# A hybrid decoder block on one core: latents loaded tile by tile over 13 slots, query evacuations in a row, other banks for the last unit's transposes

## The chip, the cores and the metric

The kernel runs on one core of a Trainium2 chip. The metric is the device time of one execution in microseconds (us); lower is better. Before the change the median of three runs is 906.58 us, between 903.97 and 908.92.

The engines are TensorE (PE, with its weight loads as PEld), VectorE (DVE), ScalarE (ACT), GpSimd (POOL) and SyncE (SP), whose queue issues nearly all transfers (DMAs). Each runs its own instructions in a fixed order; a wait of one instruction holds all behind it.

## The reference, cut to what matters

One layer on a sequence of 1024 tokens, width 1024, in float32. A normalised and modulated input is projected once; the parts of the projection feed two groups of heads.

```python
h = rms_norm(x, norm_g) * (1 + scale) + shift
proj = h @ w_in                                        # (1024, 3360)
y_rwkv = rwkv7_time_mix(proj[..., :1664], ...)         # 8 heads of 64: a recurrence over the tokens
q  = (rms_norm(c_q,  q_norm_g)  @ w_uq).reshape(..., 8, 96)   # c_q: 384 columns of proj
kv = (rms_norm(c_kv, kv_norm_g) @ w_ukv).reshape(..., 8, 128) # c_kv: 256 columns of proj
y_mla = causal softmax attention of 8 heads (64 + 32 rotary)
y = concat(y_rwkv * silu(gate_r), y_mla * silu(gate_m))
out = rms_norm(x + gate * (y @ w_out), final_g)
```

`c_q` and `c_kv` are the latents: low-rank tensors from which all queries, keys and values are made. The change is about how they are brought back from DRAM and used.

## The kernel before, in words

Large matrix products take three matmuls: each float32 operand is split into a rounded part (`h`, hi) and a rest (`l`, lo), and hi*hi, lo*hi and hi*lo are added in PSUM. A split is a cast on ACT (`split_to`, L787) and a subtraction on DVE (L790).

The work up to the attention is one loop over step groups `n` = 0 to 10 with `STEPS[n]` steps `j` each (L1019 to L1035). Each step issues pieces of the recurrence and then, by a rate per group (`RATE`), pieces of a filler that keeps PE busy:

- The recurrence is cut into 8 units, each two head pairs on 256 tokens. A unit is prepared (`prep`, `products`, `invert`), fetched and turned (`fetch`, `turn_kb`, `turn_v`, `tmat`), run through `chain` in four sequential steps of small matmuls (L690, L697, L709, L712) with evacuations on ACT, and finished in `post`: the group norm, transposes into the PSUM tile `ytps` (L761), and the affine map on ACT (L764). `invert` is a serial row of 62 small DVE instructions on a PSUM tile `W` (L609, L611), with its input `N` and output `d_w` moved through DRAM.
- The filler (`filler`) projects 24 tiles of 128 columns (`proj`, 2 halves of 24 matmuls, L165 to L167) into two PSUM banks, tag `mm`. The last ones are the latents (`latent`, evacuated into `craw` and stored to `d_c`) and four gate tiles (`evac_gate`: `tg` on ACT, L234, and DVE, L235). Then `values` makes the rotary queries (`qrope`, tiles `qrps`), the values (tiles `vps`) and the first head pair's keys and queries (`heads_qk`, tiles `qkps`).

Staging tiles of 128x512 come from one pool and tag, `e2`, with three buffers (`etile`): the evacuations of the projections, the latents read back (`cr`) and raw weights (`wqr`) all share them. Tiles of one tag are handed out in turn. A second tag of that pool, `p2`, has two buffers (`ys`, `y2`, `bv`, `gr` of `post`, and `dg` of the latents).

`latents` is a generator called twice. At (n, j) = (7, 20) it closes the left pools, loads and splits all of `cq` (three tiles of two halves, `load_c`) and loads `wqr`, the raw rotary query weights. At (8, 6) it loads and splits `ckv` (two tiles of two halves); its halves are first scaled by the row norms, which four small matmuls spread over the partitions (`dg`, `rps`, L802 to L805). It then sets `turned`, for which the filler waits before it starts `values`.

The planner of the framework orders the instructions of each engine: greedily by the order in which the program issued them, as their inputs and tile buffers come free in its model of the machine. `tc.high_priority(offset=...)` moves instructions ahead in that order; `tc.issue_after(ins)` puts the instructions of a block behind `ins` on its engine. Engines that touch one PSUM bank are ordered against each other.

PSUM has eight banks: two of `psM` (tag `mm`) and six of `psA` (`rp` twice, `rc`, `ry`, `rt`, `w`). `ytps` uses `rt`, but in the last unit (n = 7) it uses `mm`. After the loop both pools are closed, and the attention's `psQ` (`op`, `qk`) and `psB` (`s`, `tp`) take the banks.

The attention loops over 64 tiles (head pair, head, block of 128 queries): scores `sp`, a maximum, exponentials, transposes, and the product with the values. During a pair, `heads_qk` makes the next pair's keys and queries through one bank `qk`: an ACT cast of 64 rows (L851) and a DVE subtraction (L852) for each of the two heads.

## Time and profile before

| What | us |
|---|---|
| median of three runs (lowest, highest) | 906.58 (903.97, 908.92) |
| the profiled execution | 912.47 |
| its span, first to last instruction | 910.4 |
| PE busy in it | 825.5 (91%) |
| DVE, ACT, POOL busy | 558.5, 487.7, 306.6 |
| latents read back (`cr`), first and last issue | 493.3, 547.1 |
| first scores of the attention | 634.4 |

Rows of the profile name the engine, the line (L165 is line 165 of the kernel), the operation, the tile written and the tiles read, and the shape. In a timeline the first two numbers are the start and the duration in us, and the bracket gives how long the engine stood idle just before and what released it. In a table of stretches each engine has its busy time and its number of instructions; PEclk is the share of TensorE's full clock that was granted. The projections are over at about 586 us, the filler at 626 us; the attention runs from there to 813 us, and the output projection closes the kernel.

### The profile page before, as it was taken

The page shows a single profiled execution, that of the slowest core. Times are in us where ns is not written, and L with a number is a line of the kernel's source. Part 1 is how long each engine was busy: PE and PEld are TensorE (multiplying, and loading weights), DVE is VectorE, ACT ScalarE, POOL GpSimd, SP SyncE. Part 2 cuts the span into 40 slices and gives each one's busy share as a digit, 9 for nine tenths or more (in the row PEclk, how much of TensorE's full clock was granted, in tenths as well). Part 3 has the DMA queues.
Part 4 walks back from the last instruction along what each step waited for, and adds up shares of the span by engine and source line. Part 5 has one row for each costly group of instructions (what it writes and reads, how often), then busy time and mean ns, then how long its engine had stood idle before and what let it go on. Part 6 is the DMA issues. An engine that isn't in the chain of part 4 may idle for free.

```text
span 910.4 us, 16433 instructions
## 1 busy us (share of the span) xinstructions
PE 825.5 (91%) x5764; PEld 637.2 (70%) x5764; DVE 558.5 (61%) x1450; ACT 487.7 (54%) x1136; POOL 306.6 (34%) x359
## 2 busy tenths in 40 slices
PE   1798999989999999899999889997999998989996
PEld 1586777767767776576667667665777776868785
DVE  5795438367675653866666445266887877764532
ACT  2655223444564746337454563555788887772332
POOL 2311414131414321433332302234445544454440
PEclk9999989999999999999999769998899999999998
DMA  8765434523354333343333423257102121027234
GB/s 265 241 194 157 139 99 130 140 77 116 102 178 121 106 86 105 114 117 107 95 99 116 113 87 105 78 185 167 45 21 65 50 91 47 1 72 241 70 107 148
DMA packets 130562, 104.56 MB, mean 115 GB/s; under 512 B 40488, under 2 KB 108336, under 8 KB 130480
## 3 DMA queue, kind: packets, MB, share of 16 engines
q1 hardware_dynamic: 128368, 98.27, 36.6%
q0 software_dynamic: 960, 3.15, 1.7%
q10 hardware_dynamic: 1152, 2.10, 0.6%
q8 instruction: 46, 0.75, 0.4%
q14 instruction: 36, 0.29, 0.1%
HBM read 75.42 MB, written 28.05 MB: 114 GB/s over the span
## 4 chain that ended last, share of the span: by engine, by line
PE 57%; DVE 11%; ACT 11%; DMA 9%; issue 5%; POOL 4%; SPq 2%; POOLq 0%; DVEq 0%; ACTq 0%
PE mm L165 9%; PE mm L166 8%; PE mm L167 8%; DMA wor<-in_w_out 3%; PE gps L559 2%; ACT pr L1092 2%; PE tp L1103 2%; ACT PTh L1112 2%; PE rc L690 1%; PE rc L697 1%; PE rc L709 1%; DVE PTl L1113 1%; PE po L1166 1%; PE po L1167 1%; PE po L1165 1%
## 5 line engine op out<-in xcount | busy, mean ns | idle before, releaser
L165 PE MATMUL mm<-hTh,whi 128*128 128x512 f32 (+1 forms) x384 | 166.5, 433 | 1.3 <-DVE tg L235 1.3
L166 PE MATMUL mm<-hTl,whi 128*128 128x512 f32 (+1 forms) x384 | 156.2, 407 | 0.0
L167 PE MATMUL mm<-hTh,wlo 128*128 128x512 f32 (+1 forms) x384 | 156.1, 407 | 0.0
L158 POOL TENSOR_TENSOR wlo<-wraw,whi 128x512 fp32r<-128x512 f32 (+1 forms) x54 | 70.6, 1309 | 218.6 <-ACT whi L157 209.7
L165 PEld LDWEIGHTS mm<-hTh,whi 128*128 128x128 f32 (+1 forms) x384 | 72.8, 190 | 21.8 <-DVE tg L235 1.5
L167 PEld LDWEIGHTS mm<-hTh,wlo 128*128 128x128 f32 (+1 forms) x384 | 72.8, 190 | 17.1
L166 PEld LDWEIGHTS mm<-hTl,whi 128*128 128x128 f32 (+1 forms) x384 | 72.9, 190 | 15.5 <-issue 1.9
L1096 POOL TENSOR_SCALAR pr<-pr,sm 128x512 f32<-128x512 f32 (+2 forms) x96 | 55.2, 584 | 78.2 <-DVE sm L1093 49.7
L1092 ACT ACTIVATE pr<-sp,mx,rss 128x128 f32<-128x128 f32 (+3 forms) x64 | 53.4, 834 | 16.0 <-DVE mx L1085 12.9
L1113 DVE TENSOR_TENSOR PTl<-tp,PTh 128x512 fp32r<-128x512 f32 (+2 forms) x96 | 52.3, 554 | 12.8 <-ACT PTh L1112 11.1
L157 ACT CAST whi<-wraw 128x512 fp32r<-128x512 f32 (+1 forms) x54 | 32.7, 607 | 48.8 <-PE mm L166 37.2
L1084 DVE TENSOR_REDUCE mx<-sp 128x1 f32<-128x128 f32 (+3 forms) x64 | 48.1, 751 | 17.2 <-PE sp L1078 17.0
L609 DVE TENSOR_TENSOR wtmp<-W,N 128x60 f32<-128x60 f32 (+24 forms) x248 | 51.2, 206 | 10.2 <-ACT W L604 4.7
L611 DVE TENSOR_TENSOR W<-W,wtmp 128x60 f32<-128x60 f32 (+24 forms) x248 | 53.3, 215 | 5.7
L720 ACT ACTIVATE ST<-rc,eL 64x64 f32<-64x64 f32 x120 | 37.1, 309 | 29.8 <-PE rc L709 28.1
L1112 ACT CAST PTh<-tp 128x512 fp32r<-128x512 f32 (+2 forms) x96 | 44.1, 478 | 15.1 <-PE tp L1103 12.2
L1165 PE MATMUL po<-wo,yh 128*128 128x512 f32 x128 | 50.3, 393 | 0.8 <-ACT od L1139 0.8
L1166 PE MATMUL po<-wo,yh 128*128 128x512 f32 x128 | 50.4, 394 | 0.7 <-DVE wo L790 0.7
L1103 PE MATMUL tp<-cstt,pr 128*128 128x128 f32 x288 | 45.8, 280 | 5.1 <-DVE PTl L1113 2.7
L1167 PE MATMUL po<-wo,yl 128*128 128x512 f32 x128 | 50.3, 393 | 0.0
L1124 PE MATMUL op<-PTh,Vt 128*128 128x256 f32 (+1 forms) x160 | 41.9, 293 | 5.1 <-ACT od L1139 5.1
L1074 PE MATMUL sp<-kt,qt 96*128 96x512 f32 (+2 forms) x96 | 37.2, 388 | 3.0 <-ACT pr L1092 3.0
(282 smaller groups left out, 1973.7 us busy)
## 6 DMA issues: line engine op xcount, KB each, us to landing
wraw<-in_w_in SPq DMA_DIRECT2D x52, 256.0 KB, 3.3
wa<-in_w_ada SPq DMA_DIRECT2D x64, 128.0 KB, 3.4
xt<-in_x SPq DMA_DIRECT2D x8, 512.0 KB
wg<-in_w_ada SPq DMA_DIRECT2D x32, 128.0 KB, 2.7
N<-d_n SPq DMA_DIRECT2D x32, 128.0 KB, 2.7
wor<-in_w_out SPq DMA_DIRECT2D x16, 256.0 KB, 2.9
d_c<-craw SPq DMA_DIRECT2D x10, 256.0 KB, 3.0
cr<-d_c SPq DMA_DIRECT2D x10, 256.0 KB, 3.3
```

The lines of the kernel that those rows point to most:

```text
L158: G.tensor_tensor(lo[:, :, :m], raw[:, :, :m], hi[:, :, :m].bitcast(F32), ALU.subtract)
L165: T.matmul(ps[:m], lhsT=hi[:, k % 4, :m], rhs=a, start=first, stop=False)
L166: T.matmul(ps[:m], lhsT=hi[:, k % 4, :m], rhs=b, start=False, stop=False)
L167: T.matmul(ps[:m], lhsT=lo[:, k % 4, :m], rhs=a, start=False, stop=last)
L1092: A.activation(pr[:, 0:n], sp[:, 0:n], AF.Exp, scale=rss[:, i:i + 1], bias=mx[:], accum_out=sm[:])
L1096: G.tensor_scalar(pr[:, a:e], pr[:, a:e], sm[:], 1.0, ALU.mult, ALU.mult)
L1103: T.transpose(tp[:, j, :], pr[:, (j0 + j) * P:(j0 + j + 1) * P], ident)
L1112: A.copy(th[:, 0:m, bs], tp[:, 0:m])
L1113: V.tensor_tensor(tl[:, 0:m, bs], tp[:, 0:m], th[:, 0:m, bs].bitcast(F32), ALU.subtract)
L1165: T.matmul(ps, lhsT=yh[k][:, ts_], rhs=hi, start=first, stop=False)
L1166: T.matmul(ps, lhsT=yh[k][:, ts_], rhs=lo, start=False, stop=False)
L1167: T.matmul(ps, lhsT=yl[k][:, ts_], rhs=hi, start=False, stop=last)
```

## The change

Three edits.

- **Latents.** `load_c` becomes a generator. It loads one half tile, ends its slot, and splits the half loaded the slot before. For `cq` the raw halves come from a pool of their own, `crp`, with two buffers, which is closed behind them; for `ckv` they stay in `e2`. `latents` then takes 13 calls: six loads and a last split of `cq`, four loads and a last split of `ckv`, and `wqr`. The list `LAT` gives the 13 places, from (7, 20) to (8, 14); `turned` is set at the last. The weights `wqr` are asked for behind `ckv`, no longer ahead of it. Loads, casts and subtractions are the same in number.
- **Evacuations of `heads_qk`.** Both casts are issued ahead of both subtractions, where each cast was followed by its subtraction. This holds for all four head pairs.
- **Transposes of the last unit.** `ytps` of unit 7 uses bank `rt` for the first pair and bank `w` for the second, in place of the two `mm` banks.

```diff
+LAT = ((7, 20), (7, 21), (7, 23), (8, 0), (8, 1), (8, 3), (8, 6), (8, 7), (8, 8), (8, 10), (8, 11), (8, 12), (8, 14))
...
-            ps = (psM if last else psA).tile([64, 4, P], F32, tag="mm" if last else "rt", name="ytps",
-                                            bufs=2 if last else 1)
+            ps = psA.tile([64, 4, P], F32, tag="w" if last and q else "rt", name="ytps", bufs=1)
...
     def load_c(n, base, nm):
         cpool[nm] = pool(st2, nm)
+        own = ExitStack()
+        if nm == "cq":
+            crp = pool(own, "crp")
+            raw = lambda nm: crp.tile([P, HALF], F32, tag="cr", name=nm, bufs=2)
+        else:
+            raw = etile
...
+        lat[nm] = chi, clo
+        left_ = []
...
             for i in range(n):
-                t = etile("cr")
+                t = raw("cr")
                 SY.dma_start(t[:], d_c[base + i][:, hs])
-                if nm == "ckv":
-                    V.tensor_tensor(t[:], t[:], ps[:].rearrange("p j t -> p (j t)"), ALU.mult)
-                split_to(chi[i][:, hs], clo[i][:, hs], t[:])
-        return chi, clo
+                def split(t=t, i=i, hs=hs, ps=ps if nm == "ckv" else None):
+                    if nm == "ckv":
+                        V.tensor_tensor(t[:], t[:], ps[:].rearrange("p j t -> p (j t)"), ALU.mult)
+                    split_to(chi[i][:, hs], clo[i][:, hs], t[:])
+                left_.append(split)
+                if len(left_) > 1:
+                    left_.pop(0)()
+                yield
+        left_.pop()()
+        own.close()
+        yield
...
-                for s in range(2):
-                    rows = slice(s * 64, s * 64 + 64)
-                    t = dst[hp % 2]
-                    evacs[:] = [A.copy(t[0:64, s, 0, hs], ps[rows]),
-                                V.tensor_tensor(t[0:64, s, 1, hs], ps[rows], t[0:64, s, 0, hs].bitcast(F32), ALU.subtract)]
+                t = dst[hp % 2]
+                rows = [slice(s * 64, s * 64 + 64) for s in range(2)]
+                e = [A.copy(t[0:64, s, 0, hs], ps[rows[s]]) for s in range(2)]
+                e += [V.tensor_tensor(t[0:64, s, 1, hs], ps[rows[s]], t[0:64, s, 0, hs].bitcast(F32), ALU.subtract)
+                      for s in range(2)]
+                evacs[:] = e[1::2]
...
-        lat["cq"] = load_c(3, 0, "cq")
+        yield from load_c(3, 0, "cq")
+        top.close()
+        yield from load_c(2, 3, "ckv")
         lat["wr"] = [load_up(w_uqr, "q_g", 3, 0, P, "wq", etile, b1)]
-        yield
-        top.close()
-        lat["ckv"] = load_c(2, 3, "ckv")
         yield
...
-            if (n, j) == (7, 20):
+            if (n, j) in LAT:
                 next(la)
-            if (n, j) == (8, TURN[2][2]):
-                next(la)
-                turned.append(1)
+                if (n, j) == LAT[-1]:
+                    turned.append(1)
```

## The prediction

> **What bounds the kernel now.** I read the page's slices first: TensorE (PE) is busy nearly throughout, so what counts is where it is not, and where the granted clock (PEclk) falls. The busy share dips in slices 23, 24 and 28 of 40, the clock in slices 24 and 25 (from about 524 to 569 us).

> ```profile
> PE   1798999989999999899999889997999998989996
> PEclk9999989999999999999999769998899999999998
> ```

> Then the table of stretches (busy time of each engine, granted clock), cut where PE's rows change their kind:

> ```profile
> core 0: us, PE busy (x) PEld busy (x) DVE busy (x) ACT busy (x) POOL busy (x), PEclk, DMA share, GB/s
> 510.80:536.50 25.70, 18.14 (x206) 13.38 (x205) 8.38 (x28) 17.23 (x46) 5.94 (x7) 0.54 0.33 87
> 536.50:540.40 3.90, 3.90 (x9) 3.11 (x10) 3.37 (x15) 1.22 (x5) 0.12 (x1) 0.51 0.71 234
> 555.00:586.60 31.60, 31.53 (x296) 22.25 (x294) 10.43 (x34) 15.24 (x43) 5.03 (x4) 1.00 0.18 50
> 586.60:598.60 12.00, 9.71 (x86) 7.36 (x85) 5.03 (x10) 6.69 (x20) 5.37 (x7) 0.86 0.65 209
> 626.40:634.40 8.00, 2.67 (x12) 1.91 (x13) 3.87 (x7) 4.76 (x10) 3.51 (x5) 0.88 0.98 168
> 634.40:643.00 8.60, 8.27 (x31) 6.37 (x30) 5.49 (x18) 4.65 (x14) 2.38 (x6) 0.52 0.18 56
> ```

> In 510.8 to 536.5 there is not one projection matmul: PE runs only the recurrence's small ones, at 0.54. From 555.0 the same recurrence runs beside projections, busy 31.53 of 31.60 at 1.00. Why the projections stop shows in the timelines of PE, ScalarE (ACT), SyncE's queue (SPq) and VectorE (DVE):

> ```profile
> 510.23 0.39 PE L166 MATMUL mm<-hTl,whi 128*128 128x512 f32 x1
> 510.46 0.39 PE L167 MATMUL mm<-hTh,wlo 128*128 128x512 f32 x1
> 536.48 0.80 PE L165 MATMUL mm<-hTh,whi 128*128 128x512 f32 x1 [1.27 <-DVE tg L235]
> 533.02 0.62 ACT L787 CAST cqh<-cr 128x512 fp32r<-128x512 f32 x1
> 535.12 1.07 ACT L234 ACTIVATE tg<-mm 128x512 f32<-128x512 f32 x2
> 534.39 0.34 SPq L821 DMA_DIRECT2D wqr<-in_w_uqr  x1
> 533.67 0.69 DVE L790 TENSOR_TENSOR cql<-cr,cqh 128x512 fp32r<-128x512 f32 x1 [9.64 <-ACT cqh L787]
> ```

> By the code's order both PSUM banks of the projections are full at 510.5; they wait for their two `tg` evacuations, which run at 535.12. A `tg` needs one of the three `e2` buffers. At one point of the program, (7, 20), six `cr` and three `wqr` tiles are asked for from the same three buffers, ahead of the `tg`s. The third `wqr` gets its buffer at 534.39, and the `tg`s follow 0.7 us later. So the bound there is a buffer queue, not an engine. DVE shows the same: it stands 9.64 us for the last `cqh`, with unit 7's inversion (the `W` steps of L609 and L611) queued behind.

> **The change, part by part. (a) Latents tile by tile, `cq` in two tiles of its own.** Removed: nothing; ten loads, ten casts, ten subtractions and four multiplies stay, and so do the three `wqr` loads. Moved: the six `cq` loads leave `e2` for pool `crp`, and each split comes one slot after its load; the four `ckv` loads come in (8, 7) to (8, 11), the three `wqr` loads at (8, 14), behind them on SP's queue.

> What the stall costs PE: its work in 510.8 to 536.5 is 18.14 x 0.54 = 9.8 us at full rate, so 25.70 - 9.8 = 15.9 us are lost; in the next stretch another 3.90 x (1 - 0.51) = 1.9. Upper end of the gain: 17.8 us, as in the stretch from 555.0, where the mixture loses 0.07 us. Lower end on this mechanism: what DVE certainly gets back, 9.64 us, because unit 7's recurrence cannot begin before its inversion is through. I take 13.5, near the middle (13.7): the row that resembles the new state most (555.0) says all of it, but its window has no latent loads in it.

> The moved loads cost PE nothing while the projections cover them. Per latent tile there is one landing, a cast and a subtraction:

> ```profile
> L808 SPq DMA_DIRECT2D cr<-d_c x10: 319/376/695, 493.3 to 547.1; - x10
> DMA to landing us min/median/max: 2.7/3.3/3.4
> L787 ACT CAST cqh<-cr x6: 610/618/627, 506.5 to 533.0; 128x512 fp32r<-128x512 f32 x6
> L790 DVE TENSOR_TENSOR cql<-cr,cqh x6: 684/692/1731, 507.9 to 533.7; 128x512 fp32r<-128x512 f32 x6
> ```

> A round over two `crp` tiles lasts about 0.4 + 3.3 + 0.6 + 0.7 = 5.0 us, three rounds 15 us (an estimate from these rows). The first projection that needs `cq` comes after the gate projections (the stretch that begins at 586.6 now), so there are tens of us of cover; without it the 15 us would stand before it. SP's issues stay at 10 x 0.38 = 3.8 us, but a load whose tile is not free yet holds SP, and with it the inversion's transfers. POOL's three scalings of `wqr` (L824) move with their loads, past unit 5's L769, under the same cover. A cast that waits for its landing holds ACT and so the recurrence's evacuations (rival 3). `turned` moves from (8, 6) to (8, 14); the queue of projections ends only in step group 9, so this costs nothing.

> **(b) Last unit's transposes in `rt` and `w`, first evacuations in a row.** What the attention's start waits for now:

> ```profile
> 625.99 0.39 PE L834 MATMUL qkps<-cqh,wql 128*128 128x512 f32 x1
> 627.58 0.60 PE L761 MATMUL ytps<-cstt,ys 128*64 128x128 f32 x4 [1.20 <-DVE kt L852]
> 628.57 0.60 PE L761 MATMUL ytps<-cstt,ys 128*64 128x128 f32 x4 [0.39 <-DVE kt L852]
> 632.92 0.79 PE L832 MATMUL qkps<-ckvh,wkh 128*128 128x512 f32 x1 [3.75 <-ACT y L764]
> 626.36 1.06 POOL L754 TENSOR_TENSOR ys<-ys,s 128x512 f32<-128x512 f32 x1
> 629.78 0.58 ACT L851 CAST qt<-qkps 64x512 fp32r<-64x512 f32 x1 [1.59 <-DVE qt L852]
> 630.27 0.30 ACT L787 CAST wkh<-wkr 128x128 fp32r<-128x128 f32 x1
> 630.59 2.28 ACT L764 ACTIVATE y<-ytps,colt 64x256 f32<-64x256 f32 x4
> ```

> With the banks moved, the first transposes still wait for GpSimd's (POOL's) `ys`, which ends at 627.42: nothing gained there; the second group's 0.39 us goes. With two casts in a row ACT no longer stands 1.59 us between them. After the last query matmul (625.99 + 0.39 = 626.4) two casts of 0.58 end about 627.6 instead of 630.36; then the `y` group starts when the first transposes are through, 627.58 + 0.60 = 628.2, instead of 630.59: 2.4 us. Bounds: 0 (the group is held by something else as long) and 8.00 - 2.67 x 0.88 = 5.65, all of the stretch's loss. I take 2.4; late next is POOL's `ys`.

> **(c) The same order in the later pairs.** One of twelve evacuations of that kind:

> ```profile
> 650.56 0.57 ACT L851 CAST kt<-qkps 64x512 fp32r<-64x512 f32 x1
> 652.00 0.67 DVE L852 TENSOR_TENSOR kt<-qkps,kt 64x512 fp32r<-64x512 f32 x1
> 652.71 0.58 ACT L851 CAST kt<-qkps 64x512 fp32r<-64x512 f32 x1
> 653.75 0.69 DVE L852 TENSOR_TENSOR kt<-qkps,kt 64x512 fp32r<-64x512 f32 x1
> ```

> The engines alternate on one bank, each starting after the other's end. In a row saves a hand-over, but PE's wait on it is small, and the exponentials behind the second cast come up to 0.58 us later. I take 0, with 0.6 us either way.

> **Sum.** 13.5 + 2.4 + 0 = 15.9 us. The profiled execution took 912.47 us with a span of 910.4: the span would be 894.5 and that execution 896.6. The median of the runs, 906.58, lies 5.9 below it, so the median forecast is 906.58 - 15.9 = 890.7 us.

> [...] PE's clock stays low after the attention begins: 0.52 from 634.4 to 643.0, a loss of 8.27 x 0.48 = 4.0 us. After the change the longest wait before it falls from 3.75 to about 1.4 us. Whether that keeps the clock up, an earlier place shows:

> ```profile
> 592.94 0.33 PE L683 MATMUL Y<-S,rq 64*64 64x64 f32 x4 [1.61 <-ACT S L722]
> 595.25 0.63 PE L833 MATMUL qrps<-cql,wqh 128*128 128x512 f32 x1
> ```

> A wait of 1.61 us among small matmuls was followed by matmuls of 0.63 us, where 0.39 is normal; so I keep the loss in. [...]

> **The rivals.** (1) The stall moves to `ckv` and `wqr`, which still use `e2`. The second `dg` now stands behind unit 5's `bv` and `gr` in the two `p2` buffers:

> ```profile
> 546.74 0.32 SPq L738 DMA_DIRECT2D bv<-d_bv  x1
> 555.40 0.69 DVE L771 TENSOR_TENSOR gr<-y,gr 128x512 f32<-128x512 f32 x1 [1.24 <-DMA gr<-d_gr]
> ```

> From the first to the end of the second are 9.4 us, in which two `cr` hold two of the three `e2` buffers and `wqr` queues for the third, ahead of the next `tg`. One projection group of 24 matmuls covers about 5.5 us (0.23 us from start to start, the rows at 510.23 and 510.46), so PE stands 3.9 us and restarts at half clock (1.9): 5.8 us. Gain 10.1, time 896.5. Against it: one `tg` still passes on the third buffer.

> (2) No change: the recurrence keeps its pace however the projections are dealt out. Its copies of `X`:

> ```profile
> 474.23 0.26 ACT L693 COPY X<-rc 128x128 f32<-128x128 f32 x1
> 498.74 0.27 ACT L693 COPY X<-rc 128x128 f32<-128x128 f32 x1
> 519.13 0.26 ACT L693 COPY X<-rc 128x128 f32<-128x128 f32 x1
> 605.70 0.27 ACT L693 COPY X<-rc 128x128 f32<-128x128 f32 x1
> ```

> With projections beside it a step took (498.74 - 474.23) / 2 = 12.3 us; seven such steps are 85.8 us, against 605.70 - 519.13 = 86.6 now. Then (a) gives 0.8 and the time is 906.58 - 0.8 - 2.4 = 903.4. Against it: between the first two rows the last unit's products and loads ran as well, which the later steps do not have beside them.

> (3) Slower: ACT stands before each of the ten split casts until its tile lands, and everything of the recurrence queues behind. Ten landings of 3.3 us are 33 us; fully on the path the time is 906.58 - 15.9 + 33 = 923.7. It decides from the fifth exposed landing on (5 x 3.3 = 16.5 > 15.9). For it: the 9.64 us row, where one late cast held DVE. Against it: each split is placed a slot behind its load. [...]

> **How the numbers follow.** Forecast 0.52, the clock's rule 0.06, rival 1 0.20, rival 2 0.12, rival 3 0.10. A measurement tells about 0.5% (4.5 us) from no change, so faster means below 902.0: 0.52 + 0.06 + 0.20 = 0.78; within: rival 2, 0.12; slower: rival 3, 0.10. Fastest by the bounds: 17.8 + 5.65 = 23.5 us, 883.1, and with part of the clock's 4.0 us 881. Range: 881 to 905, which holds all but rival 3 and small tails; the faster cases alone lie in 881 to 898.

> **What would show it.** (a) holds if projections (L165 to L167) run between 511 and 536, the clock there is near 1.0, no DVE wait on `cqh` exceeds 3.4 us, and the second unit's inversion ends some 10 us earlier. (b) holds if the wait of 3.75 us before the second pair's first matmul falls below 2. Rival 1 shows as a gap ending at a `tg` near 545; rival 2 as full stretches with the first scores still near 632; rival 3 as ACT idle released by `cr` landings. Wrong I would be most of all if the order that the planner writes for the engines changes elsewhere: every instruction after (7, 20) is placed anew.

## The result, and the profile after

The changed kernel takes 900.24 us (median of 20 runs, 894.5 to 909.4), the kernel before 907.28 us beside it (20 runs, 903.23 to 912.74). The ratio is 0.9932, 95% interval 0.9908 to 0.9955: faster by about 6.2 us (4.1 to 8.3), where 15.9 were forecast. The profiled execution took 900.45 us with a span of 898.5. A profile shows one execution, and executions scatter by 10 us or more with the granted clock: in the changed kernel from 907.8 us at a mean clock of 0.959 to 894.5 at 0.976. A profiled execution disturbed as a whole (that of e3 below) is not read.

The page of the changed kernel: the two rows of its slices that were shown of before.

```profile
PE   1798999989999999899999999897999998989996
PEclk9999999999999999999999998898899999999999
```

The clock's 7 and 6 at slices 23 and 24 (501 to 546 us before; the prediction counts them as 24 and 25) are gone. What is left of low clock lies at slices 25 and 26 (539 to 584 us) and 28 and 29 (606 to 651). The same in stretches (columns as in the prediction's table):

```profile
core 0: us, PE busy (x) PEld busy (x) DVE busy (x) ACT busy (x) POOL busy (x), PEclk, DMA share, GB/s
505.00:530.60 25.60, 24.82 (x251) 17.85 (x252) 10.42 (x32) 18.33 (x48) 6.31 (x5) 1.00 0.48 141
530.60:550.00 19.40, 17.90 (x107) 13.03 (x106) 11.44 (x36) 9.11 (x24) 4.10 (x4) 0.82 0.30 91
...
566.00:580.00 14.00, 10.55 (x138) 7.76 (x136) 4.42 (x11) 8.42 (x23) 2.46 (x5) 0.76 0.55 162
613.90:619.90 6.00, 2.54 (x14) 1.35 (x12) 4.33 (x8) 2.88 (x6) 2.31 (x4) 1.00 1.05 171
619.90:639.90 20.00, 16.79 (x67) 12.85 (x68) 11.87 (x31) 11.59 (x32) 9.16 (x18) 0.66 0.24 60
```

The first row is the place where PE did 18.14 us of work at 0.54 before; now it does 24.82 of 25.60 at 1.00. The last two rows are the start of the attention: in its first 20 us the granted clock is 0.66. (This execution was 5.85 us ahead of the one of before already at the copy of `X` that the prediction shows at 498.74, here 492.89, which lies before the change's place; positions below are compared with such a difference taken off.)

The timelines of the changed kernel there, PE, ACT and DVE:

```profile
613.92 0.40 PE L854 MATMUL qkps<-cqh,wql 128*128 128x512 f32 x1
616.33 0.50 PE L852 MATMUL qkps<-ckvh,wkh 128*128 128x512 f32 x1 [2.02 <-ACT wkh L788]
618.38 0.50 PE L854 MATMUL qkps<-ckvh,wkl 128*128 128x512 f32 x1 [1.31 <-DVE wkl L791]
618.72 1.03 PE L762 MATMUL ytps<-cstt,ys 128*64 128x128 f32 x8
621.69 0.38 PE L1094 MATMUL sp<-kt,qt 96*128 96x256 f32 x1 [1.21 <-ACT y L765]
625.16 0.69 PE L1094 MATMUL sp<-kt,qt 96*128 96x384 f32 x1 [1.16 <-ACT pr L1112]
...
619.35 2.28 ACT L765 ACTIVATE y<-ytps,colt 64x256 f32<-64x256 f32 x4 [3.07 <-PE ytps L762]
624.56 0.46 ACT L1112 ACTIVATE pr<-sp,mx,rss 128x128 f32<-128x128 f32 x1
...
621.99 1.16 DVE L791 TENSOR_TENSOR wkl<-wkr,wkh 128x128 fp32r<-128x128 f32 x1 [3.66 <-ACT wkh L788]
623.78 0.62 DVE L1104 TENSOR_REDUCE mx<-sp 128x1 f32<-128x128 f32 x2
```

Before, the transposes (`ytps`) stood ahead of the second pair's first key matmul. Now that key matmul, which waits 2.02 us for `wkh` and 1.31 us for `wkl`, stands ahead of them, so `y` starts late: ACT waits 3.07 us for the transposes, although it came free at 616.28. On DVE the first two maxima (`mx`) stand behind the second `wkl` and the product with `gr`; the first exponential (`pr`) comes 4.7 us after the first scores (619.88).

### The profile page after: what moved, and what is told of

Same layout as the page of the kernel before. It is cut to its first block, busy times and chain, and to the rows that moved or that the text cites. A ratio compares the mean times of both kernels' runs of the same rounds, so it can differ in the third digit from the quotient of the medians.

```text
span 898.5 us, 16446 instructions
## 1 busy us (share of the span) xinstructions
PE 818.2 (91%) x5764; PEld 630.3 (70%) x5764; DVE 556.4 (62%) x1450; ACT 487.4 (54%) x1136; POOL 308.7 (34%) x359
## 4 chain that ended last, share of the span: by engine, by line
PE 61%; DVE 11%; ACT 9%; DMA 6%; issue 6%; POOL 4%; SPq 2%; POOLq 0%; ACTq 0%; DVEq 0%
PE mm L166 8%; PE mm L168 8%; PE mm L167 7%; PE po L1185 3%; PE po L1186 3%; PE po L1187 3%; PE gps L560 2%; PE tp L1123 2%; PE rc L691 1%; ACT pr L1112 1%; ACT PTh L1132 1%; PE rc L710 1%; PE rc L698 1%; PE sp L1094 1%; PE op L1144 1%
## 5 line engine op out<-in xcount | busy, mean ns | idle before, releaser
L166 PE MATMUL mm<-hTh,whi 128*128 128x512 f32 (+1 forms) x384 | 165.1, 430 | 0.0
L167 PE MATMUL mm<-hTl,whi 128*128 128x512 f32 (+1 forms) x384 | 154.7, 403 | 0.0
L166 PEld LDWEIGHTS mm<-hTh,whi 128*128 128x128 f32 (+1 forms) x384 | 71.8, 187 | 20.1 <-issue 1.2
L167 PEld LDWEIGHTS mm<-hTl,whi 128*128 128x128 f32 (+1 forms) x384 | 72.1, 188 | 15.1 <-issue 1.9
L1112 ACT ACTIVATE pr<-sp,mx,rss 128x128 f32<-128x128 f32 (+3 forms) x64 | 53.4, 835 | 15.5 <-DVE mx L1105 14.6
L1104 DVE TENSOR_REDUCE mx<-sp 128x1 f32<-128x128 f32 (+3 forms) x64 | 48.0, 751 | 14.1 <-PE sp L1098 13.6
L1132 ACT CAST PTh<-tp 128x512 fp32r<-128x512 f32 (+2 forms) x96 | 43.6, 477 | 17.6 <-PE tp L1123 15.0
```

The costliest lines, as they stand in the source:

```text
L166: T.matmul(ps[:m], lhsT=hi[:, k % 4, :m], rhs=a, start=first, stop=False)
L167: T.matmul(ps[:m], lhsT=hi[:, k % 4, :m], rhs=b, start=False, stop=False)
L1112: A.activation(pr[:, 0:n], sp[:, 0:n], AF.Exp, scale=rss[:, i:i + 1], bias=mx[:], accum_out=sm[:])
L1132: A.copy(th[:, 0:m, bs], tp[:, 0:m])
```

## The experiments

The first idea, theory T, was that (a) worked as forecast, but that the gain is given back between 565 and 614 us, where PE runs out of projections and unit 7's inversion on DVE is no earlier (559.3 against 560.9). The first four runs test it and take the change apart. The runs came in four groups, each with its own runs of the kernel before beside it: 907.03 us for e1 to e4, 906.21 for e5 to e8, 905.21 for e9 to e12, 904.23 for e13 to e16. A ratio is to the group's own before, so between groups the ratios are the safer comparison.

**e1: part (a) alone.** The changed kernel with these lines as before:

```diff
-            ps = psA.tile([64, 4, P], F32, tag="w" if last and q else "rt", name="ytps", bufs=1)
+            ps = (psM if last else psA).tile([64, 4, P], F32, tag="mm" if last else "rt", name="ytps", ...)
...
-                e = [A.copy(...) for s in range(2)]
-                e += [V.tensor_tensor(...) for s in range(2)]
+                for s in range(2):
+                    evacs[:] = [A.copy(...), V.tensor_tensor(...)]
```

> Only part (a): latents tile by tile with `cq` in two tiles of its own; the last unit's transposes and the first evacuations stay as before. Theory T (the stall of 13.7 us at 510 to 536 is gone, but unit 7's inversion on DVE is not earlier, so PE runs out of projections near 566 and some 7.5 us are given back by 614): 13.7 - 7.5 = 6.2 us below before, about 901 us, projections' last start near 565, first scores some 2.4 us later than in the changed kernel. Forecast on record for (a) alone: 13.5 us below, about 894. Rival A (the gain of the whole change comes from the transposes and the evacuations): within 2 us of before, 905 to 907.

Measured: 892.1 us, ratio 0.983 (0.9798 to 0.9863): 14.9 us below before's 907.03 by the medians. That is the forecast for (a), 13.5, and not theory T's 6. In its stretches the gap behind the projections is as in the changed kernel; the start of the attention is not:

```profile
504.10:529.70 25.60, 24.86 (x251) 17.86 (x252) 10.41 (x32) 18.35 (x48) 6.30 (x5) 1.00 0.49 141
529.70:547.00 17.30, 16.51 (x107) 12.25 (x106) 12.39 (x36) 8.99 (x24) 3.98 (x4) 0.90 0.33 102
...
563.00:577.00 14.00, 10.84 (x134) 7.81 (x133) 4.42 (x11) 8.44 (x23) 2.45 (x5) 0.66 0.54 161
610.90:616.90 6.00, 1.60 (x11) 0.80 (x9) 3.70 (x7) 3.95 (x8) 2.22 (x4) 0.87 1.04 163
616.90:636.90 20.00, 18.92 (x98) 15.18 (x99) 15.62 (x41) 14.96 (x39) 11.06 (x21) 0.87 0.31 77
```

In the first 20 us of scores the clock is 0.87 (0.66 in the changed kernel) and PE does 18.92 us of work (16.79). The rows of PE, ACT and DVE in e1:

```profile
612.68 1.24 PE L763 MATMUL ytps<-cstt,ys 128*64 128x128 f32 x8 [1.45 <-POOL ys L755]
616.85 0.44 PE L1093 MATMUL sp<-kt,qt 96*128 96x128 f32 x1 [2.93 <-DMA qt<-d_qr]
...
615.34 2.29 ACT L766 ACTIVATE y<-ytps,colt 64x256 f32<-64x256 f32 x4
618.70 0.46 ACT L1111 ACTIVATE pr<-sp,mx,rss 128x128 f32<-128x128 f32 x1
...
617.89 0.29 DVE L1103 TENSOR_REDUCE mx<-sp 128x1 f32<-128x128 f32 x1 [1.86 <-PE sp L1097]
620.35 0.29 DVE L792 TENSOR_TENSOR wkl<-wkr,wkh 128x128 fp32r<-128x128 f32 x1
```

Transposes first, maxima ahead of the second `wkl`, first exponential 1.85 us after the first scores. So parts (b) and (c) take back about 8 us of what (a) gives by the medians, 9 by the ratios.

**e2: parts (b) and (c) alone**, the same lines changed in the kernel before.

> Only parts (b) and (c): transposes of the last unit in `rt` and `w`, evacuations in a row; the latents load as before. Theory T: the first scores come 2.4 us earlier, of which the attention keeps all or nothing: 0 to 2.4 us below before, about 905 to 907. Rival A: 5 to 7 us below before, 900 to 902. Rival C (the evacuations in a row cost the attention the 3.7 us that the changed kernel loses between its first scores and its last output): 1 to 3 us above before.

Measured: 906.01, ratio 0.9984 (0.9954 to 1.0015): no change that can be told. Its rows show what became of the 2.4 us forecast for (b):

```profile
624.31 0.51 PE L831 MATMUL qkps<-ckvh,wkh 128*128 128x512 f32 x1 [2.25 <-ACT wkh L786]
626.75 1.91 PE L760 MATMUL ytps<-cstt,ys 128*64 128x128 f32 x8
...
627.84 2.28 ACT L763 ACTIVATE y<-ytps,colt 64x256 f32<-64x256 f32 x4 [3.58 <-PE ytps L760]
```

The transposes stand behind the key matmul here too, and `y` starts at 627.84. This execution was 4.0 us ahead at that copy of `X` (494.72), so that is 1.3 us later than before's 630.59, not 2.4 earlier. The first scores (628.31) were still 2.0 us earlier than before's; by the first output matmul 1.7 us of it were left.

**e3: the changed kernel, latents' subtractions on POOL; e8: the same on part (a) alone.**

```diff
-                    split_to(chi[i][:, hs], clo[i][:, hs], t[:])
+                    split_to(chi[i][:, hs], clo[i][:, hs], t[:], lo_eng="pool")
```

> The changed kernel, with the ten subtractions of the latents' splits on POOL in place of DVE; what is computed is the same. In the changed kernel unit 7's inversion runs from 521.2 to 559.5; in that stretch DVE stands about 4.1 us for casts of latents and works 7 x 0.69 = 4.9 us on such subtractions, and 2.8 us of standing lie before it. Theory T: the inversion ends 8 to 11 us earlier, PE's wait at unit 7's first `y1ps` goes, the gap behind the projections (566 to 581) is filled with the recurrence earlier, and the time falls by 4 to 7 us: 893 to 896. Rival B (the values' weights, whose fifth raw tile waits for a buffer until 574, set the gap): no change, 899 to 901. Rival D (POOL becomes late instead, its queue holds the projections' weights): slower than the changed kernel by 2 us or more.

> Part (a) alone, with the ten subtractions of the latents' splits on POOL in place of DVE. Theory T (unit 7's inversion on DVE, slowed by the latents, sets when the recurrence goes on after the projections): inversion 8 to 11 us earlier, 4 to 7 us below part (a) alone (892.1), 885 to 888. Rival: the last unit starts no earlier, because the unit before it ends near 556 and the tail of the fill is bound by PE: 890 to 893.

Measured: e3 0.9896 (0.9847 to 0.9944), which overlaps the changed kernel's interval, and whose profiled execution is the disturbed one; e8 892.79, 0.9863 (0.9828 to 0.9899), no better than e1 and not the 885 to 888 of theory T. In e8 the inversion ended 3.4 us earlier than in e1 once the difference at that `X` is taken off, not 8 to 11. The first scores came 2.0 us earlier and the end of the profiled execution 2.1 us; the medians of the runs do not show even that. As the account of the missing gain, theory T has fallen.

**e4: six raw buffers for the values' weights; e11: part (a) alone, these weights loaded first.**

```diff
-                return b2.tile([P, HALF], F32, tag="raw", name=nm, bufs=4)
+                return b2.tile([P, HALF], F32, tag="raw", name=nm, bufs=6)
```

```diff
-            lat["wr"].append(load_up(w_uqr, "q_g", 3, P, P, "wr", raws, b2))
             wv = load_up(w_v, "kv_g", 2, 0, 512, "wv", raws, b2)
+            lat["wr"].append(load_up(w_uqr, "q_g", 3, P, P, "wr", raws, b2))
```

> The changed kernel with six raw buffers in place of four for the values' weights, so that the fifth and sixth raw tile can be loaded at once (now at 574.67, behind a cast of ACT at 574.02). The order on PE is that of the changed kernel, instruction by instruction. Theory T: the load lands 5 us or more earlier and nothing changes: 899 to 901. Rival B: PE's gap between 568 and 581 shrinks by some 5 us and the time by as much: 894 to 896.

> Part (a) alone, with the two loads of the values' weights placed ahead of the three of the second rope weights in the four raw buffers, so that the values' matmuls can fill PE between 566 and 580, where it runs at 0.56 of the clock. Theory X (PE is short of ready work there, for want of the values' weights): 3 to 6 us below part (a) alone, 886 to 889. Rival (the work is only moved, because the recurrence of the last unit ends no sooner): 891 to 893.

The loads of the tile `wvr` (least, median and greatest ns, first and last start), in the changed kernel and in e4:

```profile
L841 SPq DMA_DIRECT2D wvr<-in_w_v x2: 328/375/422, 569.9 to 574.7; - x2
```

```profile
L841 SPq DMA_DIRECT2D wvr<-in_w_v x2: 422/426/430, 565.7 to 566.1; - x2
```

The second load is issued some 8 us earlier, and nothing changes: e4 898.88, 0.9914 (0.9884 to 0.9944). e11: 894.6, 0.9855 (0.9805 to 0.9905), an interval that overlaps e1's; theory X's 886 to 889 did not come. These loads do not set the end.

**e5: (a) and (b); e6: (a) and (c).** Each takes one of e1's two edits, so that with e1 and the changed kernel the four cases are there.

> The changed kernel with the evacuations of queries and keys alternating as before: parts (a) and (b) without (c). The latents alone gave 892.1, 15 us below before; with the rest 7 to 8 us of that are lost again. Theory U (the freed banks let the second pair's first key matmuls stand ahead of the last unit's transposes on PE; they wait for `wkh` and `wkl`, and the `y` group, the second `wkh`, the first maxima and exponentials queue behind them): part (b) carries the loss, about 898 to 901. Rival C (the eight casts and subtractions in a row hold `wkh` and `wkl`): the loss goes with (c), 891 to 894.

> The changed kernel with the last unit's transposes in the two `mm` banks as before: parts (a) and (c) without (b). On PE the eight transposes again stand ahead of the second pair's key matmuls. Theory U: the loss is gone, 890 to 895, and the first exponential comes within 3 us of the first scores. Rival C: 898 to 901.

Measured: e5 897.98, 0.9926 (0.9894 to 0.9957); e6 896.06, 0.9895 (0.9855 to 0.9935). Beside (a) alone, by the medians (b) costs about 6 us, (c) about 4 and both together 8; by the ratios 9, 6 and 9. The price of (b) is clear of the scatter: the intervals of e1 and e5 lie apart. That of (c) is not quite: those of e1 and e6 overlap. Theory U's 898 to 901 for (b) came out; its 890 to 895 for e6 did not.

**e7: the changed kernel, the key matmuls held behind the transposes.**

```diff
+                with ExitStack() as b_:
+                    if (k, r) == (0, QKS[0]): [b_.enter_context(tc.issue_after(i_)) for i_ in turns_[-8:]]
-                    next(qk, None)
+                    next(qk, None) if ... else None
```

> The changed kernel, all three parts, with one order imposed: the second pair's first key matmuls are issued after the last unit's eight transposes. PE's order up to the first scores differs in that alone. Theory U: transposes start when POOL's `ys` ends, the `y` group starts at once behind them instead of 3.1 us after ACT came free, first exponential 4 to 5 us earlier, 894 to 897, and if the banks were all of the matter 892. Rival C: no more than 1 us, 899 to 901. Rival D (the low granted clock of 620 to 640, 0.66, comes from the small score matmuls themselves and not from the waits): the exponentials come earlier, the clock stays under 0.7 over the first 20 us of the scores, time 898 to 901.

Measured: 900.0, 0.9931 (0.9896 to 0.9965). PE's order was repaired (first row), and it did not help:

```profile
616.48 1.06 PE L762 MATMUL ytps<-cstt,ys 128*64 128x128 f32 x8 [1.46 <-POOL ys L755]
...
622.57 1.03 DVE L791 TENSOR_TENSOR wkl<-wkr,wkh 128x128 fp32r<-128x128 f32 x1 [3.53 <-ACT wkh L788]
...
625.01 0.46 ACT L1112 ACTIVATE pr<-sp,mx,rss 128x128 f32<-128x128 f32 x1 [2.48 <-DVE mx L1105]
```

The maxima still stand behind the second `wkl` on DVE, and the first exponential comes 4.3 us after the first scores (620.67). So U, in the form of PE's order, has fallen too. Rival D has its number, and the clock over the first 20 us is 0.66 as it said; but the same score matmuls ran at 0.87 in e1, so their small size alone is not the reason.

**e9: maxima first on DVE; e10: early landings; e13: both; e12: e10 on (a) alone; e16: e9 without (c).** The two edits (the second `wkl` and the last unit's product with `gr` are put off until the first two maxima stand; the second pair's raw weights go to another pool):

```diff
+                if t + AHEAD == 1:
+                    with tc.issue_after(mx0):
+                        later.pop()()
+                        later.pop()()
```

```diff
-        wqk[1] = load_qk(1)
+        wqk[1] = load_qk(1, lambda nm: at.tile([P, 256], F32, tag='od', name=nm, bufs=4))
```

> The changed kernel, all three parts; on DVE the first two maxima (`mx`) stand ahead of the second `wkl` and of the last unit's product with `gr`, which now come behind them. Runs so far: the latents alone 892.1; with the evacuations in a row 896.1; with the banks 898.0; with both 900.2, and imposing the transposes ahead of the key matmuls on PE changed nothing (900.0). Theory V: with the banks moved the maxima stand on DVE behind the second `wkl`, whose weights land near 621 because their `e2` buffer comes free late, so the first exponential comes 5.0 us after the first scores instead of 1.6, and the matmuls meanwhile run at half clock; eight subtractions in a row (part c) make the first `wkl`, and with it that landing, later still. By V this kernel has its first exponential within 2.5 us of the first scores, the eighth score some 4 us sooner after the first (19 to 20 us instead of 23.4), and 894 to 897. Rival W (the loss comes from where the half clock happens to fall in these 20 us, not from the maxima): 898 to 901.

> The changed kernel, all three parts; the raw weights of the second pair go to four tiles of another pool (`od`), so that their loads no longer wait for an `e2` buffer. The order on DVE stays: both `wkl` and two `wql` ahead of the first maxima. Theory V: `wkr` and `wqr` are there before the last unit's `y`, nothing in front of the maxima waits for a landing, first exponential within 3 us of the first scores, 893 to 897. Rival W: 898 to 901.

> Part (a) alone, with the second pair's raw weights in four tiles of another pool (`od`). There the maxima stand ahead of the second `wkl` already. Theory V: little to gain, 890 to 893; the first key matmul of the second pair waits less. Rival (landings hold the start of the attention even there): 886 to 889.

> The changed kernel with both repairs: the first maxima ahead of the second `wkl` and of the product with `gr` on DVE, and the second pair's raw weights in four tiles of `od`. Alone, the first gave 896.0 and the eighth score 21.2 us after the first (23.4 in the changed kernel, 18.9 with part (a) alone), the second nothing (901.6, 22.3). Theory V (late maxima, made worse by late landings): eighth score by 19.5 us, 892 to 895. Theory K (what counts is how many stretches of about 3.4 us the clock stays at half after the waits before the first scores: two with part (a) alone, four in the changed kernel, five with maxima first): eighth score 21 us or later if four or more of them are seen, 896 to 900, whatever the order on DVE.

> Parts (a) and (b) without (c), with the first maxima ahead of the second `wkl` and of the product with `gr` on DVE. (a) and (b) alone gave 898.0, eighth score 21.8 us after the first. Theory V: eighth score by 19.5 us, 892 to 895. Theory K: as many half-clock stretches of 3.4 us as with (a) and (b) (four), eighth score 21 us or later, 896 to 899.

Measured: e9 896.01, 0.989 (0.9846 to 0.9934); e10 901.61, 0.995 (0.9913 to 0.9987); e12 895.58, 0.988 (0.9835 to 0.9925); e13 898.44, 0.9933 (0.9894 to 0.9971); e16 898.99, 0.9947 (0.9917 to 0.9977). The order on DVE did what it should. The first exponential in ACT's timeline, in e9 and in e13:

```profile
620.48 0.45 ACT L1119 ACTIVATE pr<-sp,mx,rss 128x128 f32<-128x128 f32 x1
```

```profile
620.98 0.46 ACT L1119 ACTIVATE pr<-sp,mx,rss 128x128 f32<-128x128 f32 x1 [1.25 <-DVE mx L1112]
```

2.0 us after the first scores in e9 (618.44) and 1.6 in e13 (619.36), as theory V wanted. The time of e9 came out as V had it (894 to 897), though its eighth score did not (21.2 us, 19 to 20 forecast). But e10, e12, e13 and e16 lie above V's ranges, e16 by 4 us with the same order on DVE as e9. In e13 PE's order is put right as well: the transposes run when `ys` ends, and PE then waits for `qt`, not for a weight.

```profile
614.03 1.06 PE L762 MATMUL ytps<-cstt,ys 128*64 128x128 f32 x8 [1.45 <-POOL ys L755]
619.36 0.45 PE L1101 MATMUL sp<-kt,qt 96*128 96x128 f32 x1 [4.27 <-DMA qt<-d_qr]
```

So with both orders put right the median stays at 898.4. Of those with part (b) the best by its median is e9, 4 us above e1 with intervals that overlap. What the length of the attention's start follows is how long the clock stays at half there. Windows of e1, of the changed kernel and of e9, cut around the half-clock stretch:

```profile
615.00:616.00 1.00, 0.00 (x0) 0.00 (x0) 0.86 (x2) 0.96 (x4) 0.00 (x0) 0.68 0.84 131
616.00:622.00 6.00, 5.15 (x18) 4.29 (x19) 2.75 (x11) 3.00 (x8) 2.29 (x4) 0.50 0.27 48
622.00:623.00 1.00, 1.00 (x5) 0.65 (x3) 0.13 (x2) 0.49 (x2) 1.00 (x3) 0.90 1.06 293
```

```profile
622.00:623.00 1.00, 0.90 (x6) 0.42 (x4) 1.00 (x1) 0.00 (x0) 1.00 (x2) 0.97 0.00 0
623.00:636.00 13.00, 11.09 (x37) 8.43 (x38) 8.29 (x25) 6.42 (x18) 5.14 (x11) 0.50 0.37 92
636.00:637.00 1.00, 1.00 (x5) 0.87 (x5) 0.73 (x4) 0.75 (x2) 0.41 (x1) 0.71 0.00 0
```

```profile
616.00:617.00 1.00, 0.70 (x2) 0.46 (x3) 0.25 (x2) 0.00 (x0) 0.00 (x0) 0.68 0.71 102
617.00:633.00 16.00, 15.15 (x56) 12.15 (x55) 8.51 (x26) 9.44 (x25) 6.24 (x13) 0.50 0.31 75
633.00:634.00 1.00, 1.00 (x6) 0.90 (x5) 0.56 (x1) 0.63 (x3) 1.00 (x3) 0.79 0.14 38
```

A microsecond at 0.68 holds 0.64 us of half clock. So e1 is at half for 0.64 + 6 + 0.20 = 6.84 us, the changed kernel for 0.06 + 13 + 0.58 = 13.64, e9 for 0.64 + 16 + 0.42 = 17.06: two, four and five times 3.41 us. In the profiled executions of e1, e6, e8, e11, e12, e13, e14 and e15 it is two such pieces, in before three, in e2, e4, e5, e7 and the changed kernel four, in e10 two and two, in e16 one and four. From the first score to the eighth after it (by the starts of `sp<-causb`, the last matmul of a score) took 17.9 to 19.1 us with two pieces, 21.2 to 23.8 with four or more (e2, where one of the four lay ahead of the scores, 19.6; before, with three, 17.6). So for this stretch theory K holds. Two pieces more are 6.8 us at half clock, 3.4 us of work, less than half of what (b) and (c) take back. And they do not order whole executions: with two pieces these took 891.0 (e1) to 902.1 us (e11), with four 894.5 (e5) to 905.6 (e2). For e13 K's 896 to 900 came out by the median, 898.44; its profiled execution had two pieces and took 18.5 us there and 892.86 in all, the fastest of its 12. How many pieces its other executions had no run shows.

**e14 and e15: (a) and (c), in a row in the first pair alone, or in the later pairs alone.** The order of the four instructions depends on `hp == 0` and on `hp > 0`.

> Parts (a) and (c), with the evacuations in a row in the first pair alone; banks as before. (a) alone 892.1, (a) and (c) 896.1. If (c) costs in the first pair (subtractions behind the casts make `wkl` later): 895 to 898. If it costs in the later pairs: 891 to 894, and the stretch from the 44th to the 52nd score takes 21.3 us as with (a) alone, not 23.2.

> Parts (a) and (c), with the evacuations in a row in the later pairs alone; banks as before. If (c) costs in the later pairs: 895 to 898, and the stretch from the 44th to the 52nd score takes about 23.2 us. If in the first pair: 891 to 894.

Measured: 896.65, 0.9913 (0.9882 to 0.9944), and 895.94, 0.9895 (0.986 to 0.993). Both lie as high as e6. From the 44th to the 52nd score after the first they took 22.8 and 22.7 us (e1 21.3, e6 23.1), so that stretch is longer even where the later pairs alternate. The traces show what makes it longer: one more piece of half clock. Stretches of before, of e6 and of e10, columns as above:

```profile
750.00:775.00 25.00, 21.23 (x132) 17.59 (x131) 18.46 (x45) 18.52 (x44) 11.17 (x18) 0.93 0.14 43
```

```profile
750.00:775.00 25.00, 22.74 (x156) 19.98 (x155) 18.23 (x51) 19.98 (x49) 14.44 (x24) 0.93 0.00 1
```

```profile
750.00:775.00 25.00, 21.86 (x160) 19.18 (x159) 19.75 (x53) 20.40 (x50) 14.40 (x24) 1.00 0.00 1
```

At 0.93 these 25 us hold 3.5 us of half clock, one piece, 1.7 us of work. Beside (a) it is there in seven of the nine kernels with (c) that are read here (the changed kernel, e4, e6, e7 with two pieces, e9, e14 and e15; not in e10 and e13) and in none of the six without (c); without (a) it is in before and in e2 alike. With one piece the stretch took 22.7 to 23.1 us, with two 24.3, with none 21.2 to 21.4. So the piece mostly goes with (c), wherever the order is changed, but why is not shown, and it is less than half of the some 4 us that (c) costs by the medians. Even these are not sure: only e14's interval lies apart from e1's, e6's and e15's do not, and e12, which has no (c), stands close by at 0.988.

## Why the prediction was right and wrong

**(a), forecast 13.5 of 9.64 to 17.8: right, 14.9 measured by itself (15.4 by the ratio).** The sign named for it is there: projections fill 505.0 to 530.6 at 1.00, and DVE's longest wait for `cqh` is 2.81 us (3.4 were allowed):

```profile
516.30 0.69 DVE L791 TENSOR_TENSOR cql<-cr,cqh 128x512 fp32r<-128x512 f32 x1 [2.81 <-ACT cqh L788]
```

The other sign failed. The inversion was to end 10 us earlier; the rows of its tile `W` before, in the changed kernel and in e1 give the start of its first and of its last step:

```profile
L611 DVE TENSOR_TENSOR W<-W,wtmp x31: 174/217/245, 522.7 to 560.9; 128x60 f32<-128x60 f32 x3, 128x28 f32<-128x28 f32 x2, 128x54 f32<-128x54 f32 x2, 128x48 f32<-128x48 f32 x2
```

```profile
L612 DVE TENSOR_TENSOR W<-W,wtmp x31: 174/216/245, 521.4 to 559.3; 128x60 f32<-128x60 f32 x3, 128x28 f32<-128x28 f32 x2, 128x54 f32<-128x54 f32 x2, 128x48 f32<-128x48 f32 x2
```

```profile
L612 DVE TENSOR_TENSOR W<-W,wtmp x31: 174/216/245, 520.4 to 556.3; 128x60 f32<-128x60 f32 x3, 128x28 f32<-128x28 f32 x2, 128x54 f32<-128x54 f32 x2, 128x48 f32<-128x48 f32 x2
```

With the 5.85 and 6.78 us taken off by which the last two executions led, it ends later than before, not earlier. The lower bound's reason (the last unit cannot begin before its inversion is through) was therefore not the one that counted. What counted is what the upper bound said: PE's projections no longer wait. e8, with an inversion that ends 3.4 us earlier than e1's, is no faster by its median. That 13.5 came so near is in part luck: it is the middle of two bounds of which one had no ground, and not all of the gain lies where the sum looked for it. In the profiled executions, with the lead taken off, e1's first scores come 10.7 us earlier than before's and its end 14.6; of the 3.9 between them the clock has most, because before has four pieces of half clock at the attention's start and near 764, and e1 has two (3.4 us of work).

**(b), forecast a gain of 2.4 of 0 to 5.65: the step that failed.** Its sentence was that the `y` group starts when the first transposes are through, and "late next is POOL's `ys`": it took the order of PE and DVE as given. In its place, beside (a), part (b) costs 6 us by the medians of e1 and e5, 9 by their ratios. The planner put the second pair's key matmuls ahead of the transposes, as e2 and the changed kernel show, and ACT stood 3.07 us for them. The sign named for (b) failed as well, if narrowly: that pair's first matmul waits 2.02 us, for `wkh`, where less than 2 was asked. The wait for `y`, which used to stand before it (3.75 us), went to the second scores (1.21 us), and on DVE the maxima came behind the second `wkl`. I had bounded the term by nothing below, because every wait that it moved looked shorter.

That these orders arose is shown; that they are the price is not. With PE's order put right the time was 900.0 (e7), with DVE's 896.0 and 899.0 (e9, e16), with both 898.4 (e13). What goes with the moved banks in all profiled executions read here but e13's is four or five pieces of half clock at the attention's start, where those with (a) and the old banks have two: 3.4 to 5.1 us of work. Why the clock stays down there, and where the rest of the price lies, stays open.

**(c), forecast 0, 0.6 either way: probably wrong.** Beside (a) the medians give it a cost of about 4 us (e1 to e6, e14, e15), but only e14's interval lies apart from e1's; 1.7 us of it can be seen as the piece of half clock in the later pairs. Without (a), (b) and (c) together move nothing (e2).

**The loss of clock at the attention's start: rightly kept in the sum.** The forecast gives 0.06 to the case that the 4.0 us lost there are gained too (the clock's rule); no run shows such a rule. What the runs showed in its place: in the changed kernel the longest wait of PE between 613.92 and the first scores is 2.02 us, and the clock then stays at half for 13.64 us; in before, behind the wait of 1.61 us at 592.94, the granted clock is 0.50 from 594.94 to 598.36. What the weighing had wrong is that the loss would stay as it was: half clock at the attention's start went from 10.2 us in before's profiled execution to 13.6, and with (a) alone fell to 6.8.

**The rivals.** (1) Part of it is there: PE waits 1.50 us for the second `dg` at 539.33, and the stretch 530.6 to 550.0 holds 17.90 x 0.82 = 14.7 us of work at full rate in 19.40, 4.7 lost where 5.8 were reckoned; in e1, with the same order there, 17.30 - 16.51 x 0.90 = 2.4. What (a) measures contains it. (2) The recurrence did keep its pace (the last unit's first copy of `X` comes 80.8 us after the copy at 492.89, before 79.5 after the one at 498.74), and the time fell all the same. (3) No landing held ACT: from 480 to 560 us its only wait before a split cast of a latent is 0.2 us, for PE (`lps`).

**The size.** Mean time by mean granted clock is 907.4 x 0.9647 = 875 us for before, 891.9 x 0.9778 = 872 for e1, 900.6 x 0.9682 = 872 for the changed kernel; for all kernels here between 871 and 876. So between e1 and the changed kernel the mean clock accounts for the whole difference; between before and the changed kernel for about half of it (at before's product the changed kernel's clock would give some 904 us, 3.3 of the 6.7). Part (a) lifts the clock by 0.013, and (b) and (c) take 0.010 back. This is an account and not yet a cause, and it holds for means: the profiled execution of the changed kernel took 900.45 us at 0.976, a product of 879. The sum asked what waits; it had no term for a change of the clock at the attention's start, where in the changed kernel's profiled execution PE's waits are 1.16 to 2.02 us and half clock lasts 13.64 us.

## What to carry to other kernels

Cost a freed buffer or bank by what it lets move ahead on the in-order engines, not only by the wait that it ends: here a key matmul moved ahead of the transposes (ACT waited 3.07 us for them) and a weight's split ahead of the first maxima (first exponential 4.7 us after the first scores, 1.85 in e1). Then test that story too: putting these orders right one by one, and both, did not bring the time of (a) alone back. At the start of the attention the half clock took 3.4 us of work where PE ran on without a wait behind its first scores (e1, waits of 1.45 and 2.93 us ahead of them), and 6.8 where waits of 1.2 us stood between the first scores (the changed kernel). When parts of a change are forecast together, measure each alone: (a) alone has the lowest median of the 16 variants run, 892.1 us, and nothing added to it made it faster.

## What the runs showed of the hardware that was not expected

```profile
620.40:631.70 11.30, 11.30 (x37) 8.78 (x38) 6.92 (x21) 6.69 (x20) 5.77 (x11) 0.50 0.40 95
```

In e1 the clock returned after 5.4 us of work without a gap (from 616.85 to 622.2). The two stretches hold the same kinds of matmul in another mixture; what brings the clock back stays open.
